# A small triangular solve moved from VectorE to GpSimd in a two-layer encoder kernel

## Chip, cores and metric

One NeuronCore of a Trainium2 chip. The metric is the device time of one execution in microseconds (us), lower is better. The engines are named as the profile names them: PE (TensorE), PEld (its weight loads), DVE (VectorE), ACT (ScalarE), POOL (GpSimd) and SP (SyncE, here a queue of DMAs).

## What is computed

Two layers of an encoder over 512 tokens of width 1024. Each layer projects the tokens, runs five mixers on the result, gates and sums them, projects once more and normalises. Four mixers are attentions. The fifth is a linear recurrence in two directions `e`, and the change lies in it:

```python
def rwkv7_step(state, inp):
    r, w, k, v, a, bb = inp
    sa = jnp.einsum('bhij,bhj->bhi', state, a)
    state = state * w[:, :, None, :] + sa[..., None] * bb[:, :, None, :] + v[..., None] * k[:, :, None, :]
    return state, jnp.einsum('bhij,bhj->bhi', state, r)
...
for e, rev in ((0, False), (1, True)):
    _, ye = lax.scan(rwkv7_step, jnp.zeros((b, B_HEADS, HEAD_DIM, HEAD_DIM), F32), xs, reverse=rev)
```

The kernel doesn't step through 512 tokens. It takes chunks of 64, and inside a chunk the term `sa` makes a triangular system. Its 32x32 diagonal blocks are inverted by substitution, 31 steps long, for all chunks and heads of a unit at once.

## The kernel before

The recurrence of a layer is cut into eight units, four pairs of heads by two directions. A unit has two halves, both generators. `early` makes the decays, the keys and, by PE (line 877), the blocks of the system; ACT copies those out of PSUM into `NS` (lines 886 and 889). `late` turns `NS` into `U` on DVE (line 949), starts `W` from an identity, and runs the substitution: per step a product `pr` (line 959) and a sum into `W` (line 961), 62 instructions a unit, each of which needs the one before. Four DVE transposes bring `W` into the diagonal blocks of `WD` (line 966), one corner of `WD` is cleared (972), two more transposes give `TN` (973), and from there PE and ACT work through the off-diagonal blocks (977, 979, 984, 986), the chunk products (1005 to 1031) and the chain of states (1038 to 1041). The diagonals of the decay, written into `A0` (tile name `AR`, line 929), belong to `early` and are read at line 1023.

The loop over units runs `late(n)` beside `early(n + 1)`, one step of each in turn, and after each step `pull(1)` takes one step of the fill: three matmuls of 512 columns (lines 149 to 151) of the gate and branch products, which have nothing to do with the recurrence. Their weights are split in two parts first, `whi` by ACT (line 135) and `wlo` by DVE (line 136).

The engines' orders are not those of the code. A scheduler works out an order for each engine when the kernel is built, and then it is fixed: each engine takes its instructions one after the other, and one that waits holds up all behind it. POOL before has little to do: DMA issues (lines 365, 434, 436) and a few clears.

Of the kernel before, what the change touches and what calls it, by code (L numbers as in the profile page):

```python
# [14 lines left out]
ALU = mybir.AluOpType  # L15
# [37 lines left out]
def encoder_kernel(ctx: ExitStack, tc: tile.TileContext, x, mem, ln_in, rel_bias, w_in, par, w_up, a_up,  # L53
                   d_lambda, w_mem, w_branch, w_gate, w_out, lnp, cst, cossin, onehot, cnt, msk, out):
    nc = tc.nc
# [26 lines left out]
    tt = nc.vector.tensor_tensor  # L82
# [19 lines left out]
    def M(n):  # L102
        o, w = _MW[n]
        return msk_t[:, o:o + w]
# [167 lines left out]
    with tc.tile_pool(name="init", bufs=1) as ip:  # L272
# [20 lines left out]
        for t in range(2):  # L293
            for j in range(2):
# [4 lines left out]
                sl = slice(t * 128, (t + 1) * 128)  # L299
# [11 lines left out]
        for i in range(2):  # L311
            ps = ps_m()
            sl = slice(i * 512, (i + 1) * 512)
# [10 lines left out]
    for l in range(L):  # L324
# [85 lines left out]
        with tc.tile_pool(name=f"att{l}", bufs=1) as at:  # L410
# [115 lines left out]
            for hp in range(4):  # L526
# [10 lines left out]
                q = q_stack(ps)  # L537
                k = k_stack(ps2)
# [71 lines left out]
            for b in range(4):  # L610
                q = qn
                g = b // 2
                of = tile_of("oc", [128, S], F32, 2)
                for i in range(2):
                    p4 = []
                    for qb in range(4):
                        ps = ps_s()
                        score(ps, q, (kh, kl), i, qb, S, g)
                        p, _ = softmax(ps, S)
# [10 lines left out]
            with tc.tile_pool(name=f"attd{l}", bufs=1) as ad:  # L630
# [12 lines left out]
                for h in range(4):  # L643
                    ps = ps_g()
                    proj(ps, l, 44 + h, hT)
                    q = q_stack(ps)
                    ps = ps_g()
                    proj(ps, l, 48 + h, hT)
                    k = k_stack(ps)
# [5 lines left out]
                    b = load_bias(8 + h)  # L655
# [25 lines left out]
            with tc.tile_pool(name=f"attm{l}", bufs=1) as am:  # L681
                kv = am.tile([128, 4, 256], F32, name="kvm", tag="kvm")
                nc.sync.dma_start(out=kv, in_=scr_kv[l].rearrange("b p t -> p b t"))
                for b in range(2):
                    ps = ps_g()
                    proj(ps, l, 60 + b, hT)
                    q = q_stack(ps)
                    k = k_stack(kv[:, b, :], 256)
                    v = v_pair(kv[:, 2 + b, :], 2)
                    of = tile_of("of", [128, S], F32, 2)  # L690
                    for i in range(2):
                        p4 = []
                        for qb in range(4):
                            ps = ps_s()
                            score(ps, q, k, i, qb, 256)
                            p, _ = softmax(ps, 256, None, (DVE, ACT)[qb % 2])
# [8 lines left out]
        with tc.tile_pool(name=f"rw{l}", bufs=1) as rp:  # L705
            def T(n, shape, bufs=1, dt=F32):
                return rp.tile(shape, dt, name=n, tag=n, bufs=bufs)
# [4 lines left out]
            def recurrence():  # L712
# [10 lines left out]
                WD = T("WD", [128, 8, 128])  # L723
# [74 lines left out]
                def early(p, e):  # L798
                    if e == 0:
                        yield from pair_start(p)  # L800
                    q = pairs[p]
                    up, k, r, v, nkk, vsw, kes = (q[n] for n in ("up", "k", "r", "v", "nkk", "vsw", "kes"))
# [37 lines left out]
                    A0 = T("AR", [128, 8, 3, 64], 2)  # L840
# [17 lines left out]
                    for h in range(2):  # L858
                        sl = slice(64 * h, 64 * h + 64)
# [4 lines left out]
                    Z = T("Z", [128, 2, 4, 128], 2)  # L864
                    OM = T("OM", [128, 2, 8, 128], 2)
                    NS = T("NS", [128, 8, 2, 32], 2)
                    mr = M("mr%d" % e).rearrange("p (o t) -> p o t", o=1).to_broadcast([128, 4, 64])
                    mmk = M("mm%d" % e).rearrange("p (o u t) -> p o u t", o=1, u=2).to_broadcast([128, 2, 2, 64])
                    for c2 in range(2):
                        pss = [ps_s(), ps_m()]  # L870
                        MB = T("MB", [128, 2, 2, 128], 1)
                        for j in range(4):
                            c = 4 * c2 + j
                            for h, ps in enumerate(pss):
                                sl = slice(64 * h, 64 * h + 64)
# [19 lines left out]
                        for h in range(2):  # L895
                            for c in range(2):
# [1 line left out]
                                mm_cols(pmv[:, j * 64:(j + 1) * 64], MB[:, h, c, :], vsw[:, 2 * c2 + c, 64 * h:64 * h + 64])  # L898
                        nc.scalar.copy(Z[:, :, 2 * c2:2 * c2 + 2, 64:128],
                                       pmv[:, 0:256].rearrange("p (h c j) -> p h c j", h=2, j=64))  # L900
                    q[e] = (Z, NS, OM, A0)
                    yield

                    act(comp, comp, AF.Exp, scale=-hc)
# [20 lines left out]
                    for h in range(2):  # L925
                        sl = slice(64 * h, 64 * h + 64)
                        idb = ident[sl, 64 * h:64 * h + 64].rearrange("p (o t) -> p o t", o=1).to_broadcast([64, 8, 64])
                        gcb = gc[sl].rearrange("p (c o) -> p c o", o=1).to_broadcast([64, 8, 64])
                        tt(A0[sl, :, h, :], idb, gcb, ALU.mult)
                    if e == 0:  # L930
                        nc.vector.tensor_copy(kes, ke)
                    else:
# [7 lines left out]

                def late(p, e):
                    q = pairs[p]
                    Z, NS, OM, A0 = q[e]
                    vsw = q["vsw"]


                    U = T("U", [128, 32, 32], 1)
                    nd = NS[:, :, e, :]
                    nc.vector.transpose(out=U, in_=bass.AP(nd.tensor, nd.offset, [list(nd.ap[0]), [1, 32], [64, 8], [0, 4]]))
                    W = T("W", [128, 8, 32], 1)  # L950
                    nc.scalar.copy(W, M("wid").rearrange("p (a b) -> p a b", b=32))
                    for s in range(31, 0, -1) if e == 0 else range(31):
                        if e == 0:
                            t8, rsl, n = slice(s // 4, 8), slice(0, s), s
                        else:
                            t8, rsl, n = slice(0, s // 4 + 1), slice(s + 1, 32), 31 - s
                        nt = t8.stop - t8.start
                        pr = T("pr", [128, 80], 1)[:, :nt * n].rearrange("p (a b) -> p a b", b=n)
                        tt(pr, W[:, t8, s:s + 1].to_broadcast([128, nt, n]),  # L959
                           U[:, s:s + 1, rsl].to_broadcast([128, nt, n]), ALU.mult)  # L960
                        tt(W[:, t8, rsl], W[:, t8, rsl], pr, ALU.add)  # L961
                        if s % 4 == 2:
                            yield
                    for g in range(4):
                        gs = slice(32 * g, 32 * g + 32)
                        nc.vector.transpose(out=WD[gs, :, gs].rearrange("p k (a b) -> p a k b", b=4), in_=W[gs])

                    TN, RB = U[:, 0:8, :], U[:, 8:16, :]
                    sg = [slice(32 * g, 32 * g + 32) for g in (e, 2 + e)]
                    tg = [slice(32 * g, 32 * g + 32) for g in (1 - e, 3 - e)]  # L970
                    for u in range(2):
                        nc.vector.memset(WD[tg[u], :, sg[u]], 0.0)
                        nc.vector.transpose(out=TN[sg[u]], in_=WD[sg[u], :, sg[u]])
                    ps = ps_t()
                    for k in range(8):
# [16 lines left out]
                    n = 0  # L992
# [119 lines left out]
        with tc.tile_pool(name=f"out{l}", bufs=1) as op:  # L1112
# [27 lines left out]
            for t in range(4):  # L1140
                sl = slice(t * 128, (t + 1) * 128)
# [131 lines left out]
```

## Time and profile before

| | |
|---|---|
| median of three runs | 2314.18 us (2313.76 to 2317.56) |
| profiled execution | 2311.92 us, of which the span is 2310.1 us |
| busy share of the span | PE 96%, PEld 73%, DVE 75%, ACT 55%, POOL 3% |
| mean granted clock of PE | 0.991 |

The span reaches from the first to the last instruction. A busy share is the time in which an engine had an instruction in flight. PE's matmuls overlap, so that its share stays high even where they start late.

### The profile page before, as it was taken

The numbers are of one execution on the slowest core, as the hardware profiler recorded it, in microseconds if no ns is written. First come the engines' busy times: TensorE is split into PE (matmuls) and PEld (weight loads), VectorE is DVE, ScalarE is ACT, GpSimd is POOL, SyncE is SP. The second block draws the span as 40 slices with busy tenths as digits, with TensorE's granted clock in tenths as the row PEclk, the third lists the DMA queues.
The fourth block names the chain that finished last, engine by engine and source line by source line (L and its number), as shares of the span: only waits on it lengthen the run. The fifth ranks groups of instructions, "written<-read, shape, count | busy, mean of one in ns | idle before, by whom it ended". The sixth has DMA issues, their size and how long they took to land.

```text
span 2310.1 us, 36289 instructions
## 1 busy us (share of the span) xinstructions
PE 2206.5 (96%) x13056; PEld 1690.5 (73%) x13056; DVE 1733.0 (75%) x4236; ACT 1273.5 (55%) x2785; POOL 60.9 (3%) x119
## 2 busy tenths in 40 slices
PE   6999999999999999999999999999999999999998
PEld 5877777777677777776877777777677777777676
DVE  7676886576889797965567778766778979878455
ACT  3555666675655565544235656666675646555440
POOL 0000000000000000000000000000000000000000
PEclk9999999999999999999999999999999999999999
DMA  7733123332222221315334321232312222222350
GB/s 261 230 95 86 64 76 96 105 95 80 73 79 70 93 77 60 108 51 190 101 116 104 94 64 62 94 99 83 114 60 92 74 65 94 72 93 67 100 180 37
DMA packets 112612, 222.58 MB, mean 96 GB/s; under 512 B 13304, under 2 KB 23288, under 8 KB 112048
## 3 DMA queue, kind: packets, MB, share of 16 engines
q1 hardware_dynamic: 102000, 196.14, 26.5%
q0 software_dynamic: 10432, 24.12, 4.1%
q8 instruction: 103, 1.69, 0.3%
q14 instruction: 77, 0.63, 0.1%
HBM read 188.71 MB, written 28.36 MB: 94 GB/s over the span
## 4 chain that ended last, share of the span: by engine, by line
PE 53%; issue 17%; DVE 17%; ACT 7%; DMA 5%; POOL 0%; SPq 0%; DVEq 0%; POOLq 0%; ACTq 0%
PE pg L150 7%; PE pg L151 7%; PE pg L149 7%; PE pf L149 5%; PE pf L150 4%; PE pf L151 4%; PE psc L443 3%; DVE pr L959 2%; DVE W L961 2%; PE po L488 2%; PE pt L469 2%; DVE wlof L136 1%; PE psc L151 1%; PE psc L150 1%; PE psc L149 1%
## 5 line engine op out<-in xcount | busy, mean ns | idle before, releaser
L150 PE MATMUL pg<-hT,whir 128*128 128x512 f32 (+1 forms) x912 | 366.0, 401 | 0.5 <-DVE hT L176 0.5
L149 PE MATMUL pg<-hT,whir 128*128 128x512 f32 (+1 forms) x912 | 364.4, 400 | 1.9 <-DVE q L424 1.6
L151 PE MATMUL pg<-hT,wlor 128*128 128x512 f32 (+1 forms) x912 | 364.3, 399 | 1.7 <-DVE wlor L136 1.7
L136 DVE TENSOR_TENSOR wlor<-wrawr,whir 128x512 fp32r<-128x512 f32 x240 | 163.7, 687 | 123.2 <-ACT whir L135 114.5
L135 ACT CAST whif<-wrawf 128x512 fp32r<-128x512 f32 (+1 forms) x272 | 164.6, 606 | 149.9 <-PE pf L150 87.4
L135 ACT CAST whir<-wrawr 128x512 fp32r<-128x512 f32 x240 | 147.5, 618 | 178.4 <-PE pg L150 111.9
L149 PE MATMUL pf<-hT,whif 128*128 128x512 f32 x512 | 223.0, 435 | 8.9 <-DVE y L385 5.0
L136 DVE TENSOR_TENSOR wlof<-wrawf,whif 128x512 fp32r<-128x512 f32 (+1 forms) x272 | 181.6, 669 | 48.3 <-ACT whif L135 43.1
L150 PE MATMUL pf<-hT,whif 128*128 128x512 f32 x512 | 208.3, 407 | 0.0
L151 PE MATMUL pf<-hT,wlof 128*128 128x512 f32 x512 | 207.7, 406 | 0.0
L151 PEld LDWEIGHTS pg<-hT,wlor 128*128 128x128 f32 x912 | 172.2, 189 | 40.6 <-DVE wlor L136 4.2
L149 PEld LDWEIGHTS pg<-hT,whir 128*128 128x128 f32 x912 | 172.4, 189 | 38.8 <-ACT whir L135 2.6
L150 PEld LDWEIGHTS pg<-hT,whir 128*128 128x128 f32 x912 | 172.2, 189 | 37.8 <-issue 3.6
L176 DVE TENSOR_TENSOR pT<-pt,pT 128x512 fp32r<-128x512 f32 x176 | 114.2, 686 | 36.3 <-ACT pT L175 34.9
L175 ACT CAST pT<-pt 128x512 fp32r<-128x512 f32 x176 | 94.6, 588 | 63.7 <-PE pt L469 62.6
L149 PEld LDWEIGHTS pf<-hT,whif 128*128 128x128 f32 x512 | 97.5, 190 | 41.2 <-DVE gt L387 10.7
L469 PE MATMUL pt<-cst,p 128*128 128x128 f32 x704 | 118.6, 273 | 0.0
L151 PEld LDWEIGHTS pf<-hT,wlof 128*128 128x128 f32 x512 | 97.3, 190 | 22.4 <-issue 1.6
L959 DVE TENSOR_TENSOR pr<-W,U 128x60 f32<-128x60 f32 (+24 forms) x496 | 103.8, 209 | 11.9
L150 PEld LDWEIGHTS pf<-hT,whif 128*128 128x128 f32 x512 | 98.0, 191 | 18.9 <-issue 3.9
L961 DVE TENSOR_TENSOR W<-W,pr 128x60 f32<-128x60 f32 (+24 forms) x496 | 102.8, 207 | 10.8
L469 PEld LDWEIGHTS pt<-cst,p 128*128 128x128 f32 x704 | 89.7, 141 | 27.3 <-DVE p L460 2.9
(324 smaller groups left out, 4836.9 us busy)
## 6 DMA issues: line engine op xcount, KB each, us to landing
wrawr<-in_w_in_dram SPq DMA_DIRECT2D x224, 256.0 KB, 2.8
wrawf<-in_w_gate_dram SPq DMA_DIRECT2D x160, 256.0 KB, 2.8
o<-scr_o POOLq DMA_DIRECT2D x28, 512.0 KB, 4.5
wrawf<-in_w_branch_dram SPq DMA_DIRECT2D x48, 256.0 KB, 2.7
bias<-scr_toe SPq DMA_DIRECT2D x24, 448.0 KB, 3.3
scr_o<-os SPq DMA_DIRECT2D x20, 512.0 KB, 3.1
wrawf<-in_w_in_dram SPq DMA_DIRECT2D x32, 256.0 KB, 3.2
wrawr<-in_w_out_dram SPq DMA_DIRECT2D x32, 256.0 KB, 3.0
```

The lines of the kernel that those rows point to most:

```text
L135: nc.scalar.copy(hi, raw)
L136: tt(lo, raw, f(hi), ALU.subtract)
L149: mm(ps, ah, bh, start=(i == 0), stop=False)
L150: mm(ps, ah, bl, start=False, stop=False)
L151: mm(ps, al, bh, start=False, stop=(i == n - 1))
L175: nc.scalar.copy(hi, src)
L176: tt(lo, src, f(hi), ALU.subtract)
L443: mm(ps[:, :nk], q[:, i, sl], part[:, i if g is None else g, :nk], start=(j == 0), stop=(j == 1))
L469: nc.tensor.transpose(pt[:, qb * 128:(qb + 1) * 128], p4[qb][:, kb * 128:(kb + 1) * 128], ident)
L488: mm(po, vwin(kb), pT[:, b, :], start=(kb == 0 and b == 0), stop=(kb == nkb - 1 and b == 1))
L959: tt(pr, W[:, t8, s:s + 1].to_broadcast([128, nt, n]), U[:, s:s + 1, rsl].to_broadcast([128, nt, n]), ALU.mult)
L961: tt(W[:, t8, rsl], W[:, t8, rsl], pr, ALU.add)
```

## The change

The substitution and the transpose that feeds it move from the start of `late` into the middle of `early`, right behind the last `NS`, and its 62 instructions go to GpSimd. `late` fetches the result. The transposes that fetch it get a pin: each may not be issued ahead of the DVE instruction traced before it. The clear of the corner and the two diagonals of `A0` go to GpSimd as well. The yields inside the substitution are gone, eight or so a unit, and with them as many steps of the fill in the code's order.

```diff
@@ early @@
+                    U = T("U", [128, 32, 32], 1)
...
-                        tt(pr, W[:, t8, s:s + 1].to_broadcast([128, nt, n]),
+                        nc.gpsimd.tensor_tensor(pr, W[:, t8, s:s + 1].to_broadcast([128, nt, n]),
                            U[:, s:s + 1, rsl].to_broadcast([128, nt, n]), ALU.mult)
-                        tt(W[:, t8, rsl], W[:, t8, rsl], pr, ALU.add)
-                        if s % 4 == 2:
-                            yield
+                        nc.gpsimd.tensor_tensor(W[:, t8, rsl], W[:, t8, rsl], pr, ALU.add)
+                    q[e] = (Z, NS, OM, A0, U, W)
+                    yield
...
-                        tt(A0[sl, :, h, :], idb, gcb, ALU.mult)
+                        nc.gpsimd.tensor_tensor(A0[sl, :, h, :], idb, gcb, ALU.mult)
...
@@ late @@
-                    Z, NS, OM, A0 = q[e]
+                    Z, NS, OM, A0, U, W = q[e]
...
-                        nc.vector.transpose(out=WD[gs, :, gs].rearrange("p k (a b) -> p a k b", b=4), in_=W[gs])
+                        tc.keep_in_program_order(
+                            nc.vector.transpose(out=WD[gs, :, gs].rearrange("p k (a b) -> p a k b", b=4), in_=W[gs]))
...
-                        nc.vector.memset(WD[tg[u], :, sg[u]], 0.0)
+                        nc.gpsimd.memset(WD[tg[u], :, sg[u]], 0.0)
```

In the changed file line 905 is the transpose into `U` (949 before), 915 and 917 are `pr` and `W` (959 and 961), 946 the diagonals (929), 965 the transposes into `WD` (966), 971 the clear, 972 the transposes into `TN` (973) and 976 the first matmuls that need them (977).

The first place is DVE's order in the third unit of layer 0, from the transpose into `U`. Before, the substitution's instructions follow it on the same engine, with other work let in between them:

```order
1065 L949 STREAM_TRANSPOSE U<-NS 128x1024
1066 L959 TENSOR_TENSOR pr<-W,U 128x31
1067 L961 TENSOR_TENSOR W<-W,pr 128x31
1068 L959 TENSOR_TENSOR pr<-W,U 128x30
1069 L961 TENSOR_TENSOR W<-W,pr 128x30
1070 L959 TENSOR_TENSOR pr<-W,U 128x29
```

Now eight instructions (rows with x2 are two) stand between that transpose and the fetch of the result:

```order
929 L905 STREAM_TRANSPOSE U<-NS 128x1024
930 L136 TENSOR_TENSOR wlof<-wrawf,whif 128x512
931 L1040 COPY ST_5177<-pt 64x64
932 L1050 TENSOR_TENSOR SY<-pt,SY 64x256 x2
933 L136 TENSOR_TENSOR wlof<-wrawf,whif 128x512
934 L387 SCALAR_TENSOR_TENSOR gt<-gt,pf 128x512
935 L136 TENSOR_TENSOR wlof<-wrawf,whif 128x512
936 L965 STREAM_TRANSPOSE WD<-W 32x8x8x4 x4
937 L972 STREAM_TRANSPOSE U<-WD 32x256 x2
```

What moved is the whole substitution, and the fetch now follows the transpose closely. Over the eight units of a layer 18, 13, 7, 9, 10, 9, 9 and 11 instructions stand between them.

The second place is PE, in the same unit, where it first needs the result. These are the last rows ahead of it and the first behind:

```order
2490 L149 MATMUL pf<-hT,whif 128x512
2491 L150 MATMUL pf<-hT,whif 128x512
2492 L151 MATMUL pf<-hT,wlof 128x512
2493 L149 MATMUL pf<-hT,whif 128x512
2494 L150 MATMUL pf<-hT,whif 128x512
2495 L976 MATMUL pt<-U,NS 32x32
2496 L151 MATMUL pf<-hT,wlof 128x512
2497 L1066 MATMUL pm<-ys,cst 128x512
2498 L976 MATMUL pt<-U,NS 32x32 x15
```

Between the last block of the system (line 877) and the first matmul of line 976 stood 192, 324, 319, 274, 270, 280, 283 and 204 matmuls in the eight units of a layer before. Now 72, 94, 92, 92, 88, 93, 85 and 105 stand there, of which 48, 27, 52, 40, 48, 43, 45 and 53 have 512 columns.

The third place is POOL, at the head of the same unit's substitution (the rows ahead of it end the unit before):

```order
179 L915 TENSOR_TENSOR pr<-W,U 128x8
180 L917 TENSOR_TENSOR W<-W,pr 128x8
181 L946 TENSOR_TENSOR AR<-cst,gc 64x8x64 x2
182 L971 MEMSET WD 32x8x32 x2
183 L365 DMA o<-scr_o 128x1024 x4
184 L915 TENSOR_TENSOR pr<-W,U 128x31
185 L917 TENSOR_TENSOR W<-W,pr 128x31
```

POOL's queue was nearly empty here; now the diagonals, the clears and the issues of four reloads (line 365, which wait for PE to be done with the tiles that they overwrite) stand between two substitutions.

## Rows read from the trace of the kernel before

**Rows 1.** The page: busy time, share of the span and instructions of each engine.

```profile
span 2310.1 us, 36289 instructions
PE 2206.5 (96%) x13056; PEld 1690.5 (73%) x13056; DVE 1733.0 (75%) x4236; ACT 1273.5 (55%) x2785; POOL 60.9 (3%) x119
```

**Rows 2.** Windows, the two recurrences: width, then busy us (instructions), clock, DMA share, GB/s.

```profile
core 0: us, PE busy (x) PEld busy (x) DVE busy (x) ACT busy (x) POOL busy (x), PEclk, DMA share, GB/s
584.00:1050.00 466.00, 451.81 (x3465) 336.67 (x3464) 384.31 (x1073) 260.44 (x630) 6.48 (x12) 0.99 0.24 76
...
1700.00:2150.00 450.00, 435.28 (x3323) 325.25 (x3322) 382.42 (x1066) 256.83 (x629) 6.49 (x12) 0.99 0.25 77
```

**Rows 3.** Timeline of PE, fill matmuls: start, duration, engine, line, operation, tiles.

```profile
587.83 0.39 PE L149 MATMUL pf<-hT,whif 128*128 128x512 f32 x1
588.06 0.39 PE L150 MATMUL pf<-hT,whif 128*128 128x512 f32 x1
588.29 0.39 PE L151 MATMUL pf<-hT,wlof 128*128 128x512 f32 x1
588.52 0.40 PE L149 MATMUL pf<-hT,whif 128*128 128x512 f32 x1
```

**Rows 4.** Groups by line: what leaves DVE (busy us, mean ns of one).

```profile
L959 DVE TENSOR_TENSOR pr<-W,U 128x60 f32<-128x60 f32 (+24 forms) x496 | 103.8, 209 | 11.9
L961 DVE TENSOR_TENSOR W<-W,pr 128x60 f32<-128x60 f32 (+24 forms) x496 | 102.8, 207 | 10.8
L929 DVE TENSOR_TENSOR AR<-cst,gc 64x512 f32<-64x512 f32 x32 | 21.9, 684 | 0.5
L972 DVE MEMSET WD<- 32x256 f32 x32 | 8.7, 272 | 2.6
```

**Rows 5.** Timeline of DVE: the substitution back to back, layer 0's last unit.

```profile
989.72 0.19 DVE L959 TENSOR_TENSOR pr<-W,U 128x31 f32<-128x31 f32 x1
989.94 0.19 DVE L961 TENSOR_TENSOR W<-W,pr 128x31 f32<-128x31 f32 x1
...
1012.98 0.17 DVE L961 TENSOR_TENSOR W<-W,pr 128x8 f32<-128x8 f32 x1
```

**Rows 6.** Groups by line: what POOL does now.

```profile
L434 POOL DMA_DIRECT2D kh<-kh x40 | 20.7, 517 | 989.8 <-ACT kh L433 805.8 <-DVE wlof L136 125.4 <-PE pt L501 38.9
L321 POOL CAST msk<-mk 128x1152 bf16<-128x1152 f32 x1 | 2.0, 1954 | 21.2 <-DMA par<-in_par_dram 21.2
L724 POOL MEMSET WD<- 128x1024 f32 x2 | 1.9, 973 | 70.0 <-DVE cf L716 35.2 <-DMA scr_o<-os 34.8
L728 POOL MEMSET ST<- 128x128 f32 x4 | 0.8, 229 | 0.0
L1263 POOL MEMSET const-float32-0.0<- 128x1 f32 x1 | 0.1, 98 | 0.2 <-issue 0.2
```

**Rows 7.** Timeline: from the system's blocks to `U`, and from `W` to PE.

```profile
581.09 1.16 PE L877 MATMUL pm<-AR,BK 64*128 64x128 f32 x8
582.51 0.25 ACT L886 COPY NS<-pm 32x128 f32<-32x128 f32 x1
...
583.26 0.20 ACT L889 COPY NS<-pm 32x64 f32<-32x64 f32 x1
584.16 1.24 DVE L949 STREAM_TRANSPOSE U<-NS 128x1024 f32<-128x1024 f32 x1
...
625.33 1.82 DVE L966 STREAM_TRANSPOSE WD<-W 32x256 f32<-32x256 f32 x4
627.18 0.90 DVE L973 STREAM_TRANSPOSE U<-WD 32x256 f32<-32x256 f32 x2
627.67 0.24 PE L977 MATMUL pt<-U,NS 32*32 32x32 f32 x2 [1.92 <-DVE U L973]
```

**Rows 8.** Groups by line: DVE's work that now stands between transpose and fetch.

```profile
L136 DVE TENSOR_TENSOR wlof<-wrawf,whif 128x512 fp32r<-128x512 f32 (+1 forms) x272 | 181.6, 669 | 48.3 <-ACT whif L135 43.1 <-PE pf L151 4.3
L1041 DVE COPY ST<-pt 64x64 f32<-64x64 f32 x112 | 25.4, 227 | 14.7 <-ACT ST L1040 10.9
L1051 DVE TENSOR_TENSOR SY<-pt,SY 64x256 f32<-64x256 f32 x32 | 13.5, 423 | 1.8 <-PE pt L1038 1.2
```

**Rows 9.** Waits of PE for the result: us in total, times, longest.

```profile
PE pt L977 <- DVE U L973: 5.3, 4, 1.9
```

More of the change, by code (lines that the diff above doesn't have):

```diff
@@ L900, in early @@
                                        pmv[:, 0:256].rearrange("p (h c j) -> p h c j", h=2, j=64))
-                    q[e] = (Z, NS, OM, A0)
+                    U = T("U", [128, 32, 32], 1)
+                    nd = NS[:, :, e, :]
+                    nc.vector.transpose(out=U, in_=bass.AP(nd.tensor, nd.offset, [list(nd.ap[0]), [1, 32], [64, 8], [0, 4]]))
+                    W = T("W", [128, 8, 32], 1)
+                    nc.scalar.copy(W, M("wid").rearrange("p (a b) -> p a b", b=32))
+                    for s in range(31, 0, -1) if e == 0 else range(31):
+                        if e == 0:
+                            t8, rsl, n = slice(s // 4, 8), slice(0, s), s
+                        else:
+                            t8, rsl, n = slice(0, s // 4 + 1), slice(s + 1, 32), 31 - s
+                        nt = t8.stop - t8.start
+                        pr = T("pr", [128, 80], 1)[:, :nt * n].rearrange("p (a b) -> p a b", b=n)
+                        nc.gpsimd.tensor_tensor(pr, W[:, t8, s:s + 1].to_broadcast([128, nt, n]),
+                           U[:, s:s + 1, rsl].to_broadcast([128, nt, n]), ALU.mult)
+                        nc.gpsimd.tensor_tensor(W[:, t8, rsl], W[:, t8, rsl], pr, ALU.add)
+                    q[e] = (Z, NS, OM, A0, U, W)
                     yield
@@ L942, in late @@
                     q = pairs[p]
-                    Z, NS, OM, A0 = q[e]
+                    Z, NS, OM, A0, U, W = q[e]
                     vsw = q["vsw"]
[L947 to L958, printed above, removed]
-                        tt(pr, W[:, t8, s:s + 1].to_broadcast([128, nt, n]),
-                           U[:, s:s + 1, rsl].to_broadcast([128, nt, n]), ALU.mult)
-                        tt(W[:, t8, rsl], W[:, t8, rsl], pr, ALU.add)
-                        if s % 4 == 2:
-                            yield
                     for g in range(4):
                         gs = slice(32 * g, 32 * g + 32)
-                        nc.vector.transpose(out=WD[gs, :, gs].rearrange("p k (a b) -> p a k b", b=4), in_=W[gs])
+                        tc.keep_in_program_order(
+                            nc.vector.transpose(out=WD[gs, :, gs].rearrange("p k (a b) -> p a k b", b=4), in_=W[gs]))
                     TN, RB = U[:, 0:8, :], U[:, 8:16, :]
```

## Prediction

> **What bounds the kernel now.** I read the page first: PE is in flight for 96% of the span, DVE for 75%, POOL for 3% [rows 1]. That says little about whether PE is full, so I next looked at starts instead of durations in the timeline. Fill matmuls of 512 columns take 0.39 us each but start 0.23 us apart [rows 3]; back to back they overlap, and 0.23 us is the price of one. Then I took the windows of the two recurrences, the only stretches that the change touches: 466 and 450 us, with PE idle 14.2 and 14.7 us, DVE busy 384 and 382 us (82% and 85%), POOL 6.5 us each [rows 2]. So PE sets the pace there too, DVE is close behind, and all that PE could win back from idleness is 28.9 us, 1.2% of the kernel. PE's waits confirm that the substitution costs it little today: it waits 5.3 us in all, four times, for the transposes that hand the result over [rows 9]. The reason stands in the order: 72 to 105 matmuls stand now, and stood 192 to 324 before, between a unit's last system block and the first matmul that needs the inverse. The long stretch hid a long substitution. The last unit of layer 0 shows how long: from 989.72 to 1013.15 us, 23.4 us with other DVE work in between, where neighbours start 0.22 us apart [rows 5].
>
> **What DVE loses.** 103.8 + 102.8 us of substitution, 21.9 us of diagonals and 8.7 us of clears [rows 4]: 237 us, which takes it from 766 to 529 us of the 916 us in both recurrences, 58%. The gain is what of PE's 28.9 us of idleness was DVE's doing. Some of it is latency from hand to hand that stays, so I take half, 14 us; the ends are 0 and 29 us.
>
> **What the substitution costs on POOL.** 62 instructions, each behind the one before, of 8 to 76 elements a partition; over the 31 steps `nt` times `n` adds up to 1560, 50 on average. No tensor operation with two inputs runs on POOL in this trace, so the price comes from neighbours [rows 6]. A MEMSET of 128 elements takes 0.229 us and one of 1024 takes 0.973 us: 0.83 ns an element and 0.12 us fixed. The CAST of 1152 elements takes 1.954 us: less the fixed part, 1.59 ns for each element read and written. Two inputs read one after the other at that rate make 50 x 2 x 1.59 ns = 0.16 us. DVE's neighbours leave 0.03 us between the end of one and the start of the next [rows 5]. Together 0.31 us. The MEMSET that gave the fixed part reads nothing, and starting two reads is on top, so I take 0.35 us, and 62 x 0.35 = 21.7 us a unit. The low end is the smallest MEMSET, 0.098 us, with 50 elements at 0.83 ns and 0.03 us between: 0.17 us, 10.5 us a unit. The high end is the dearest thing POOL does now, a DMA issue of 0.517 us, with 0.03 us: 0.55 us, 34 us a unit. DVE itself would need 62 x (0.21 + 0.03) = 15 us [rows 4, 5].
>
> The Trainium skill (GPSIMD Engine Reference, section "Performance versus the Vector engine") puts a two-input elementwise operation on GpSimd at about 2.6 cycles an element, about twice VectorE's time, and advises against such work there. By that rate, 50 elements take 0.11 us in place of my 0.16 to 0.20 us, the estimate is 0.26 us an instruction, 16 us a unit, and the sum below would end near 2374 us. No row here can show it.
>
> **How long PE can go without it.** By the order, about 90 matmuls stand between the last system block and the first matmul of line 976, half of them (44.5 on average) of 512 columns: 44.5 x 0.23 = 10.3 us. The other 45 I price by the eight of line 877 that take 1.16 us, 0.27 us of it the last one's own run, so 0.11 us apart [rows 7]: 5.0 us. One us is for small waits of its own, as PE has them now. That makes 16.3 us.
>
> In that time must pass: the copies into `NS`, 0.95 us from the first to the end of the last; the transpose into `U`, 1.24 us; the substitution; four transposes, 1.82 us; the first of two more, 0.44 us; and some 0.35 us of handing over [rows 7]. That is 4.8 us and the substitution.
>
> So PE stands still for the substitution's time less 11.5 us: with 21.7 us, 10.2 us a unit. DVE stands at the pinned fetch meanwhile: it has 7 to 18 instructions ahead of it, mostly of 0.67, 0.42 or 0.23 us [rows 8], 5.8 us on average, and is there first. Behind it wait the weight splits (line 136), so PE would soon starve even if its own next matmul were another. PE takes its instructions in order, so nothing overlaps the wait, and the fill that was meant to hide it is only done later. With 16 units: 163 us. The pin itself costs nothing beyond that, since the fetch can't start before the last sum anyway.
>
> **The smaller parts.** The diagonals on POOL, by the same rates 0.12 + 512 x 2 x 1.59 ns = 1.75 us each, two a unit, stand behind the substitution in six units of eight and are read at line 1022, after two rounds PE to ACT and the chunk products; that cover is some 6 us. Without it the price would be 3.5 us a unit. The clears, 0.3 us each, and the issues of the reloads, 4 x 0.52 us as for line 434, ahead of two units a layer, stand ahead of the substitution and wait for PE, at places near the last system block. I price them at nothing and bound them by 2 us in eight units, 16 us. The missing yields change which fill step stands where, not how many there are: nothing.
>
> **The sum.** The profiled execution took 2311.9 us, its span 2310.1 us, and the median lies 2.3 us above it. 2311.9 + 163 - 14 = 2461; with the 2.3 us, 2463 us, 6.4% slower.
>
> **The rivals.**
> - *POOL is quick enough* (the other side). If an instruction takes less than 0.185 us with its wait, the substitution fits in 11.5 us, PE never waits, and DVE's relief is all that is left: 2300 to 2285 us. Break-even with a gain of 14 us is at 12.4 us a unit, 0.20 us an instruction. For it speaks the low bound; against it, that POOL would have to beat DVE's 0.24 us.
> - *DVE and POOL hold each other up.* If a POOL instruction can't run while DVE reads two operands from SBUF, then the 5.8 us of DVE work ahead of the fetch come on top of the substitution, until DVE itself stands still: 16 x 5.8 = 93 us, 2556 us. The before trace can't tell, as POOL has no such work in it. The Trainium skill (SBUF — State Buffer, section "SBUF: two separate sides") states that rule: a VectorE instruction with two SBUF inputs and a GpSimd one that reads SBUF exclude each other for a whole instruction.
> - *An instruction costs POOL what a DMA issue does*, 0.55 us: 34 - 11.5 = 22.7 us a unit, 363 us, 2663 us.
> - *It does nothing that counts*: the wait and the relief cancel, 0.19 to 0.21 us an instruction, 2310 to 2319 us.
>
> **How the numbers follow.** The forecast's own case, 0.26 to 0.42 us an instruction, 2380 to 2525 us, gets 0.50; with the exclusion 0.20; the dearest POOL 0.11; quick POOL 0.15; cancelled 0.04. Differences under 0.2% (4.6 us) are about what a measurement can't tell from none. The range, 2300 to 2620 us, leaves out a tenth at each side: the better part of the quick case, and the worst of the dear one. Faster 0.15, same 0.04, slower 0.81; the likeliest case alone spans 2380 to 2525 us.
>
> **What the profile after would show.** POOL busy some 300 us more, its lines 915 and 917 starting 0.3 to 0.4 us apart, and a unit's 62 in 19 to 26 us. DVE near 1500 us busy, with idle time ahead of line 965 that is put down to POOL. PE waiting at line 976 for the transposes of 972, sixteen times, 10 us each, with the windows of the two recurrences some 75 us longer apiece and all other windows as they were. If the lines of DVE with two SBUF inputs grow, or POOL's spacing differs between DVE busy and DVE idle, the exclusion is real. I am wrong if POOL's spacing is under 0.2 us, or if PE finds more to do ahead of line 976 than the count of matmuls says, so that its waits there stay short of the substitution less 11.5 us.

## The result, and the profile after

The changed kernel takes 2588.01 us (2587.35 to 2592.86, four runs) against 2315.87 us in the same session: 1.118 times as long, with an interval of 1.1161 to 1.1199. The forecast had 2463 us in a range from 2300 to 2620: slower, as forecast, but by 272 us and not by 149.

The page of the kernel after, its span, its busy shares and the granted clock in 40 slices, beside [rows 1]:

```profile
span 2585.8 us, 36330 instructions
PE 2258.3 (87%) x13056; PEld 1735.2 (67%) x13056; DVE 1563.5 (60%) x3180; ACT 1272.0 (49%) x2785; POOL 420.0 (16%) x1175
PEclk9999999998888888899999999999968898888999
```

DVE is busy 170 us less and POOL 359 us more. TensorE's share falls from 96% to 87%, and in the two recurrences the granted clock leaves the nines. The next rows are windows of layer 0, the recurrence up to its last output and then what is left of the fill behind it, and the two of layer 1 (columns as in [rows 2]):

```profile
540.00:1137.00 597.00, 472.73 (x3502) 355.93 (x3503) 317.99 (x579) 279.82 (x674) 185.82 (x538) 0.87 0.19 58
1137.00:1268.00 131.00, 120.59 (x505) 93.59 (x504) 62.70 (x100) 47.99 (x85) 1.06 (x2) 1.00 0.49 155
1800.00:2400.00 600.00, 476.27 (x3471) 358.34 (x3472) 313.41 (x576) 278.11 (x671) 186.31 (x542) 0.86 0.18 57
2407.00:2538.00 131.00, 121.15 (x508) 93.97 (x507) 60.75 (x97) 45.69 (x81) 1.06 (x2) 1.00 0.43 139
```

PE is in flight for 473 of 597 us, DVE for 318, POOL for 186: no engine is full, so they wait for one another. Measured from a layer's first recurrence instruction to the first normalising step behind the fill, the layers took 595.9 and 598.7 us before and 729.9 and 737.5 us now. That is 134 and 139 us more, 273 in all, of the 276 us between the two profiled spans: nearly the whole loss lies there. What ended the waits of PE, and below of DVE (total us, times, longest), beside [rows 9]:

```profile
PE pt L976 <- DVE U L972: 139.5, 12, 17.7
PE pt L1037 <- DVE ST L1040: 85.7, 18, 12.8
```

```profile
DVE WD L965 <- POOL W L917: 218.4, 16, 17.0
```

DVE stands sixteen times, once a unit, for POOL's last sum. PE stands sixteen times for 10 to 18 us as well, ten times at line 976 and six at line 1037 (the other waits in these two rows are short). One unit shows the first kind. These are the timeline rows of PE in the seventh unit of layer 0 (start, length, then instruction, in brackets the idle time before it):

```profile
1001.46 0.61 PE L877 MATMUL pm<-AR,BK 64*128 64x128 f32 x4
...
1018.14 0.40 PE L796 MATMUL psc<-lowr,uphi 128*128 128x512 f32 x1
1032.96 0.31 PE L976 MATMUL pt<-U,NS 32*32 32x32 f32 x2 [14.43 <-DVE U L972]
...
1035.51 0.63 PE L150 MATMUL pf<-hT,whif 128*128 128x512 f32 x1
1035.94 0.63 PE L151 MATMUL pf<-hT,wlof 128*128 128x512 f32 x1
1036.37 0.63 PE L149 MATMUL pf<-hT,whif 128*128 128x512 f32 x1
```

The same stretch on DVE and then on POOL:

```profile
1005.34 1.24 DVE L905 STREAM_TRANSPOSE U<-NS 128x1024 f32<-128x1024 f32 x1
1006.60 0.23 DVE L1040 COPY ST<-pt 64x64 f32<-64x64 f32 x1
1006.86 0.69 DVE L136 TENSOR_TENSOR wlof<-wrawf,whif 128x512 fp32r<-128x512 f32 x1
1008.22 0.69 DVE L136 TENSOR_TENSOR wlof<-wrawf,whif 128x512 fp32r<-128x512 f32 x1 [0.66 <-ACT whif L135]
...
1013.52 0.80 DVE L389 TENSOR_TENSOR y<-y,gt 128x512 f32<-128x512 f32 x1
1030.62 1.82 DVE L965 STREAM_TRANSPOSE WD<-W 32x256 f32<-32x256 f32 x4 [16.31 <-POOL W L917]
1032.48 0.90 DVE L972 STREAM_TRANSPOSE U<-WD 32x256 f32<-32x256 f32 x2
```

```profile
1006.72 0.24 POOL L915 TENSOR_TENSOR pr<-W,U 128x31 f32<-128x31 f32 x1 [19.77 <-DVE U L905]
1007.03 0.63 POOL L917 TENSOR_TENSOR W<-W,pr 128x31 f32<-128x31 f32 x1
1007.74 0.24 POOL L915 TENSOR_TENSOR pr<-W,U 128x30 f32<-128x30 f32 x1
1008.06 0.25 POOL L917 TENSOR_TENSOR W<-W,pr 128x30 f32<-128x30 f32 x1
1008.39 0.61 POOL L915 TENSOR_TENSOR pr<-W,U 128x29 f32<-128x29 f32 x1
...
1010.40 0.30 POOL L917 TENSOR_TENSOR W<-W,pr 128x54 f32<-128x54 f32 x1
...
1030.38 0.21 POOL L917 TENSOR_TENSOR W<-W,pr 128x8 f32<-128x8 f32 x1
```

The chain is read off directly: POOL runs from 1006.72 to 1030.59 us, the fetch starts at 1030.62, PE's first user at 1032.96. PE had stopped at 1018.5, about 16.5 us after the last system block, and DVE, done at 1014.3, stood ready for the fetch for 16.31 us.

In three units of eight a layer PE meets the second kind of stand. It stops ahead of line 1037, the state chain of the unit before, whose DVE copy is queued behind the fetch. PE and then DVE in the sixth unit:

```profile
932.79 0.40 PE L151 MATMUL pf<-hT,wlof 128*128 128x512 f32 x1
945.35 0.80 PE L1037 MATMUL pt<-ST,PE 128*128 128x128 f32 x2 [12.16 <-DVE ST L1040]
```

```profile
944.16 0.88 DVE L965 STREAM_TRANSPOSE WD<-W 32x256 f32<-32x256 f32 x2 [12.48 <-POOL W L917]
945.07 0.23 DVE L1040 COPY ST<-pt 64x64 f32<-64x64 f32 x1
```

After a stand PE is slow for a while. In the PE rows above, fill matmuls start 0.43 us apart behind the stand, where they started 0.23 us apart in [rows 3]. The windows from ahead of that stand to its end, and two stretches behind, have the granted clock in the third column from the right:

```profile
1004.00:1018.40 14.40, 13.83 (x105) 10.40 (x103) 6.78 (x13) 7.32 (x19) 9.57 (x28) 1.00 0.20 56
1018.40:1033.00 14.60, 0.17 (x2) 0.04 (x2) 2.24 (x6) 0.47 (x2) 9.53 (x35) 0.58 0.00 1
1033.00:1050.00 17.00, 17.00 (x122) 11.63 (x124) 13.42 (x21) 10.85 (x21) 2.60 (x2) 0.66 0.11 32
1050.00:1064.00 14.00, 12.63 (x93) 9.88 (x93) 12.08 (x25) 9.78 (x29) 0.00 (x0) 0.92 0.28 92
```

Between the full level (1.00, 2.4 GHz) and the half one (0.50, 1.2 GHz), 0.66 means 11.6 of 17 us at the half level and 0.92 another 2.2 us of 14. So some 14 us of work ran at half clock behind that stand. It is one of the longer ones: by the same record of the clock it is 4 to 17 us behind the sixteen stands, 9 on average; work at half clock takes nearly twice its time (0.43 against 0.23 us).

From the starts of all of PE's matmuls, with the price of each kind taken from before, the 273 us come apart like this. Gaps of over 1 us grow by 229 us; the sixteen stands are 215 of them. Matmuls that start later than their price while the clock is at its half level take 77 us more. The small waits in between shrink by 34 us, which I put down to DVE's relief. 229 + 77 - 34 = 272. The last two terms depend on where late starts are sorted: a second count, with a median price for each tile and shape and every late start of over 1 us taken as a gap, gives 229 + 69 - 26.

### The profile page after: what moved, and what is told of

Same layout as the page of the kernel before. It is cut to its first block, busy times and chain, and to the rows that moved or that the text cites. A ratio compares the mean times of both kernels' runs of the same rounds, so it can differ in the third digit from the quotient of the medians.

```text
span 2585.8 us, 36330 instructions
## 1 busy us (share of the span) xinstructions
PE 2258.3 (87%) x13056; PEld 1735.2 (67%) x13056; DVE 1563.5 (60%) x3180; ACT 1272.0 (49%) x2785; POOL 420.0 (16%) x1175
## 4 chain that ended last, share of the span: by engine, by line
PE 49%; issue 20%; POOL 13%; DVE 8%; ACT 6%; DMA 3%; SPq 0%; DVEq 0%; POOLq 0%; ACTq 0%
POOL W L917 6%; PE pg L149 6%; PE pg L150 6%; PE pg L151 6%; POOL pr L915 6%; PE pf L149 4%; PE pf L151 4%; PE pf L150 4%; PE psc L443 2%; PE po L488 2%; PE pt L469 2%; PE psc L149 1%; PE psc L151 1%; PE psc L150 1%; PE pt L1004 1%
## 5 line engine op out<-in xcount | busy, mean ns | idle before, releaser
L149 PE MATMUL pf<-hT,whif 128*128 128x512 f32 x512 | 228.9, 447 | 14.1 <-DVE gt L387 8.8
L150 PE MATMUL pf<-hT,whif 128*128 128x512 f32 x512 | 211.4, 413 | 0.0
L434 POOL DMA_DIRECT2D kh<-kh x40 | 20.7, 517 | 992.8 <-ACT kh L433 805.6
L915 POOL TENSOR_TENSOR pr<-W,U 128x60 f32<-128x60 f32 (+24 forms) x496 | 150.6, 304 | 164.2 <-DVE U L905 126.6
L917 POOL TENSOR_TENSOR W<-W,pr 128x60 f32<-128x60 f32 (+24 forms) x496 | 157.4, 317 | 38.8
L965 DVE STREAM_TRANSPOSE WD<-W 32x256 f32<-32x256 f32 x64 | 27.9, 436 | 219.5 <-POOL W L917 218.4
L976 PE MATMUL pt<-U,NS 32*32 32x32 f32 x512 | 20.9, 235 | 139.8 <-DVE U L972 139.5
L149 PEld LDWEIGHTS pf<-hT,whif 128*128 128x128 f32 x512 | 100.4, 196 | 46.0 <-DVE gt L387 15.9
L1037 PE MATMUL pt<-ST,PE 128*128 128x128 f32 x224 | 50.5, 308 | 86.1 <-DVE ST L1040 85.7
```

Of the source, the lines that this page charges most:

```text
L149: mm(ps, ah, bh, start=(i == 0), stop=False)
L150: mm(ps, ah, bl, start=False, stop=False)
L915: nc.gpsimd.tensor_tensor(pr, W[:, t8, s:s + 1].to_broadcast([128, nt, n]), U[:, s:s + 1, rsl].to_broadcast([128, nt, n]), ALU.mult)
L917: nc.gpsimd.tensor_tensor(W[:, t8, rsl], W[:, t8, rsl], pr, ALU.add)
```

## The experiments

Three theories were put to the test. **A**: GpSimd's chain is too long for the distance between the transpose into `U` and the fetch, so DVE stands at the fetch, PE behind DVE, and the half clock follows. **B**: it is the place and the form (early half, pin, missing yields), not the engine. **C**: GpSimd and VectorE shut each other out. Differences are to the kernel before in the same session (medians 2311.8 to 2312.8 us).

| run | time us | to before | ratio, interval |
|---|---|---|---|
| dve_early | 2364.25 | +52 | 1.021 [1.0188, 1.0232] |
| no_pin | 2587.72 | +276 | 1.1185 [1.1163, 1.1206] |
| small_only | 2326.53 | +15 | 1.0053 [1.0034, 1.0072] |
| lag8 | 2370.27 | +58 | 1.0242 [1.0221, 1.0263] |
| half_chain | 2443.08 | +131 | 1.0565 [1.0539, 1.0591] |
| pool_late | 2489.32 | +177 | 1.0766 [1.0739, 1.0793] |
| dve_early_y | 2333.18 | +21 | 1.0091 [1.007, 1.0112] |
| no_yield | 2366.02 | +54 | 1.0239 [1.0213, 1.0265] |
| pool_early_y | 2528.75 | +216 | 1.0921 [1.0884, 1.0959] |
| lag8_dve | 2354.14 | +42 | 1.0178 [1.0158, 1.0199] |
| lag14_dve | 2369.79 | +57 | 1.0241 [1.0223, 1.026] |
| mixed | 2364.98 | +52 | 1.0225 [1.02, 1.025] |

**The engine alone (dve_early).** The changed kernel with the substitution's two lines back on VectorE, still early, without yields, and with a pinned fetch:

```diff
-                        nc.gpsimd.tensor_tensor(pr, W[:, t8, s:s + 1].to_broadcast([128, nt, n]),
+                        tt(pr, W[:, t8, s:s + 1].to_broadcast([128, nt, n]),
                            U[:, s:s + 1, rsl].to_broadcast([128, nt, n]), ALU.mult)
-                        nc.gpsimd.tensor_tensor(W[:, t8, rsl], W[:, t8, rsl], pr, ALU.add)
+                        tt(W[:, t8, rsl], W[:, t8, rsl], pr, ALU.add)
```

> The substitution's 62 instructions go back to VectorE but stay in the early half, behind the pinned fetch; diagonals and clears stay on GpSimd. If the length of the substitution on GpSimd against PE's work ahead of the fetch is the cause (theory A), VectorE's 62 x 0.24 us, spread out again by the scheduler, leave 77 to 134 matmuls of 512 columns ahead of the first user, and the time is 2295 to 2330 us. If the pin or the new place in the code is the cause (B), it stays above 2450 us. If it is the two engines holding each other up at SBUF (C), it is as under A.

Measured 2364 us: 220 of the 272 us go with the engine, and no stand of over 2.1 us is left in the recurrences. At the fetch's user PE now waits:

```profile
PE pt L976 <- DVE U L972: 8.3, 12, 1.4
```

So B alone can't be the main cause. But A had expected the kernel before back, and 52 us stayed; the next runs look for them.

**The pin (no_pin).** The changed kernel with `tc.keep_in_program_order(...)` taken off the fetch.

```diff
-                        tc.keep_in_program_order(
-                            nc.vector.transpose(out=WD[gs, :, gs].rearrange("p k (a b) -> p a k b", b=4), in_=W[gs]))
+                        nc.vector.transpose(out=WD[gs, :, gs].rearrange("p k (a b) -> p a k b", b=4), in_=W[gs])
```

> The changed kernel without the pin on the four fetching transposes. A: the built order differs in the last unit of each layer alone, so 2575 to 2600 us. B, the pin holds VectorE back: below 2450 us.

2587.72 against 2588.01 us: the pin costs nothing.

**The yields (no_yield, dve_early_y).** First the kernel before without the yields in its substitution, then `dve_early` with them put back:

```diff
                        tt(W[:, t8, rsl], W[:, t8, rsl], pr, ALU.add)
-                        if s % 4 == 2:
-                            yield
```

> The kernel before with the seven yields between the substitution's steps left out, nothing else. If yields cost by themselves: 2340 to 2370, with the leftover fill of a layer longer by 15 to 25 us. If they cost nothing, as the prediction has it: 2305 to 2322.

```diff
                         tt(W[:, t8, rsl], W[:, t8, rsl], pr, ALU.add)
+                        if s % 4 == 2:
+                            yield
```

> The changed kernel with the substitution on VectorE in the early half, as in the run of that edit (2364), and with the seven yields between its steps put back. If the missing yields cost the 52 us that run lay above the kernel before (fill that finds no place in the recurrence and runs alone behind it): 2305 to 2335, and the stretch between the last y copy and the first z step falls from 127 to about 78 us a layer. If it is the early place or the small parts on GpSimd: 2350 to 2370, that stretch unchanged.

There are eight yields a unit (every fourth of the 31 steps), not the seven that the recorded texts name. Leaving them out costs the kernel before 54 us, and to put them back gives `dve_early` 31 us. The windows show how, `dve_early` first and then with the yields (recurrence of layer 0, then the fill left over):

```profile
538.00:1034.00 496.00, 468.40 (x3520) 348.53 (x3518) 397.45 (x1077) 284.45 (x680) 32.18 (x44) 0.98 0.22 71
1034.00:1161.00 127.00, 116.78 (x489) 91.19 (x490) 62.18 (x101) 46.12 (x82) 1.06 (x2) 1.00 0.48 157
```

```profile
540.00:1071.00 531.00, 504.24 (x3712) 380.43 (x3711) 423.00 (x1113) 296.12 (x703) 33.39 (x47) 0.98 0.23 74
1071.00:1146.00 75.00, 71.56 (x299) 56.71 (x298) 44.33 (x71) 33.73 (x59) 0.55 (x2) 0.98 0.62 211
```

With the yields PE does 190 matmuls more inside the recurrence and as many fewer behind it. The recurrence grows by 35 us, the rest shrinks by 52. The fill is the same; where it covers the recurrence's waits it costs less than alone.

**The small parts (small_only).** The kernel before, with only the clears and the decay diagonals on GpSimd:

```diff
-                        tt(A0[sl, :, h, :], idb, gcb, ALU.mult)
+                        nc.gpsimd.tensor_tensor(A0[sl, :, h, :], idb, gcb, ALU.mult)
...
-                        nc.vector.memset(WD[tg[u], :, sg[u]], 0.0)
+                        nc.gpsimd.memset(WD[tg[u], :, sg[u]], 0.0)
```

> The kernel before with its diagonals and corner clears alone on GpSimd. A: nothing waits for them, VectorE is 30 us lighter: 2295 to 2318 us. C: thirty-two diagonals of 1.29 us each hold VectorE's two-input instructions up, by up to 41 us: 2320 to 2355 us.

They cost 15 us, though DVE is 30 us freer: 8 us above A's range and within C's. The trace shows C at work. Line 823, a two-input instruction that now often starts beside a diagonal on POOL, takes twice its time, first before and then in `small_only`:

```profile
L823 DVE TENSOR_TENSOR tmp<-tmp 128x512 f32<-128x512 f32 x16 | 11.0, 684 | 0.0
L823 DVE TENSOR_TENSOR tmp<-tmp 128x512 f32<-128x512 f32 x16 | 21.1, 1318 | 0.0
```

Twelve of the sixteen take 1.53 us in place of 0.68. That is 10 us of DVE's time; whether it makes up the 15 us was not shown. With the yields' 31 us the small parts leave 6 of the 52 us of `dve_early` to its early place and the rest, if the three add up.

**Half of the chain (half_chain).** The changed kernel with every second step left out:

```diff
-                    for s in range(31, 0, -1) if e == 0 else range(31):
+                    for s in range(31, 0, -2) if e == 0 else range(0, 31, 2):
```

> Leaves out every second of the 31 steps of the substitution (16 remain, so the inverse is wrong); place, pin and missing yields are those of the changed kernel. GpSimd's chain falls from 23.5 to about 12 us a unit, VectorE's work does not change. Theory A (the stand is the chain less what TensorE has in hand, and the half clock follows the stand): the stands of 10 to 18 us shrink to at most 3 us, the half clock behind them goes, time 2300 to 2360. Theory B (the early place, with the pin and without the yields, costs TensorE its fill whatever the chain's length): above 2500. Theory C (GpSimd and VectorE shut each other out, each busy microsecond alike): half of the 272 us goes, 2440 to 2470.

2443 us, in the range of C and 83 us above that of A. The stands did not shrink to 3 us either: four a layer at line 976 are still 5 to 11 us long. But A's range had left out what the yields and the small parts cost, not known then: with 31 to 54 and 15 us on top it would have been 2346 to 2429. The chain fell from 23 to 24 us to 12 to 13 in most units, and DVE's stand from 218 us to:

```profile
DVE WD L965 <- POOL W L917: 81.5, 14, 10.3
```

That is 8.6 us less a unit for a chain 11 us shorter: the stand follows the chain, though not one for one. A and C can't be told apart by the time of this run.

**The engine in the old place (pool_late).** The kernel before with the two lines on GpSimd, late, with the yields:

```diff
-                        tt(pr, W[:, t8, s:s + 1].to_broadcast([128, nt, n]),
+                        nc.gpsimd.tensor_tensor(pr, W[:, t8, s:s + 1].to_broadcast([128, nt, n]),
                            U[:, s:s + 1, rsl].to_broadcast([128, nt, n]), ALU.mult)
-                        tt(W[:, t8, rsl], W[:, t8, rsl], pr, ALU.add)
+                        nc.gpsimd.tensor_tensor(W[:, t8, rsl], W[:, t8, rsl], pr, ALU.add)
```

> The kernel before with one edit: the substitution's two lines run on GpSimd, in the late half where they stood, with the yields between the steps; clears, diagonals and fetch stay on VectorE, unpinned. Theory A (cover decides, not the engine): the order has 80 to 168 fill matmuls of 512 columns between the last matmul that feeds the chain and its first user in seven units of eight, 18 to 39 us against a chain of 23.5; in the first unit of a layer only 45. So 2320 to 2390, with a stand of about 10 us left in unit 0 of each layer. Theory B (GpSimd itself, through the two engines' shared memory port, sets the time): above 2500, as in the changed kernel.

2489 us: A as it was put, with the count of fill matmuls ahead of PE's first user, missed by 100 us, and B's bound by 11. The timeline of DVE, and then of PE, in one of its units says why:

```profile
716.35 0.70 DVE L136 TENSOR_TENSOR wlof<-wrawf,whif 128x512 fp32r<-128x512 f32 x1 [1.58 <-ACT whif L135]
730.59 1.82 DVE L966 STREAM_TRANSPOSE WD<-W 32x256 f32<-32x256 f32 x4 [13.54 <-POOL W L961]
732.52 0.27 DVE L972 MEMSET WD<- 32x256 f32 x1
732.82 0.76 DVE L1023 TENSOR_TENSOR PE<-pt,AR 128x256 f32<-128x256 f32 x2
```

```profile
718.78 0.39 PE L150 MATMUL pf<-o,whif 128*128 128x512 f32 x1
733.30 1.98 PE L1031 MATMUL pt<-UV,OM 128*64 128x64 f32 x32 [14.13 <-DVE PE L1023]
```

PE wasn't waiting for the inverse. It waited for line 1023, a product of the unit before, which doesn't need the fetched result and stood behind the fetch in DVE's queue. Only two of the sixteen stands here, those of each layer's first unit, are at the result's own user. By the order only 10 to 16 DVE instructions stand between the transpose into `U` and the fetch here, as in the changed kernel (7 to 18). So the cover that counts is that in DVE's queue.

**More room ahead of the fetch (lag8, lag8_dve, lag14_dve).** Empty yields ahead of the fetch in the changed kernel: eight, as many as the substitution had, then eight with the small parts back on DVE, then fourteen likewise.

```diff
                     vsw = q["vsw"]
+                    for _ in range(8):
+                        yield
                     for g in range(4):
```

> The changed kernel, with eight empty steps of the late half ahead of the fetch, so that 56 to 215 matmuls of 512 columns stand ahead of its first user (27 to 53 before). A: 24 us of substitution are covered in nearly all units, the waits of 14 us go, and PE's clock stays up: 2285 to 2330 us. C: the substitution costs the same wherever it is fetched, above 2450 us.

```diff
-                        nc.gpsimd.tensor_tensor(A0[sl, :, h, :], idb, gcb, ALU.mult)
+                        tt(A0[sl, :, h, :], idb, gcb, ALU.mult)
+                    for _ in range(8):
+                        yield
-                        nc.gpsimd.memset(WD[tg[u], :, sg[u]], 0.0)
+                        nc.vector.memset(WD[tg[u], :, sg[u]], 0.0)
```

> The changed kernel with eight empty yields ahead of the fetch, as in the earlier run of that edit (2370), and with the corner clears and decay diagonals back on VectorE. If these small parts cost GpSimd's chain its time: the stand in unit 0 of each layer shrinks from 12 to about 6 us, and the 15 us that they cost alone go: 2330 to 2355. If they are free beside the covered chain: 2365 to 2375.

```diff
-                    for _ in range(8):
+                    for _ in range(14):
                         yield
```

> As the run before it with fourteen empty yields: 56 to 77 instructions between gather and fetch in VectorE's queue in six units of eight, 18 to 36 in the first and the last unit of a layer. If the stands are all that GpSimd costs: TensorE's waits of over 4 us behind the fetch go but for unit 0 and unit 7, 2305 to 2335. If the shared port costs VectorE as much as it is relieved, or the later fetch makes the next steps late: 2340 to 2380, no better than eight.

Eight yields put 26 to 67 DVE instructions between the two, and 214 of the 272 us are gone; the time is still 40 us above A's range, and 80 below C's. DVE stands at the fetch in each layer's first unit alone. PE at the fetch's user:

```profile
PE pt L978 <- DVE U L974: 24.4, 5, 12.3
```

The small parts are worth 16 us again. Fourteen yields are 16 us slower than eight, in the second range of that expectation: the stands in the middle units were gone with eight already, that of the first unit falls from over 12 us to 8.2 and 8.8, the last unit has one of 9.1 us, and a new one comes where a layer's recurrence ends, shown below. What else was seen is the price of GpSimd's instructions, here in `lag8`:

```profile
L917 POOL TENSOR_TENSOR W<-W,pr 128x60 f32<-128x60 f32 (+24 forms) x496 | 182.2, 367 | 38.3
L915 POOL TENSOR_TENSOR pr<-W,U 128x60 f32<-128x60 f32 (+24 forms) x496 | 173.7, 350 | 304.7 <-DVE U L905 267.1
```

and in the changed kernel:

```profile
L917 POOL TENSOR_TENSOR W<-W,pr 128x60 f32<-128x60 f32 (+24 forms) x496 | 157.4, 317 | 38.8
L915 POOL TENSOR_TENSOR pr<-W,U 128x60 f32<-128x60 f32 (+24 forms) x496 | 150.6, 304 | 164.2 <-DVE U L905 126.6
```

The same instructions take 0.05 us longer where DVE works beside them and not stands at the fetch, and a unit's chain is 24.8 to 34.8 us long, not 23 to 24 (30 in the first); the longest has three DMA issues (line 365) in it as well. C is real, then, but small where DVE stands.

**Yields in GpSimd's chain (pool_early_y).** The changed kernel with the eight yields between the steps:

```diff
                         nc.gpsimd.tensor_tensor(W[:, t8, rsl], W[:, t8, rsl], pr, ALU.add)
+                        if s % 4 == 2:
+                            yield
```

> The changed kernel with one edit: the seven yields between the substitution's steps are back, in the early half, the steps still on GpSimd. The order then has 48 to 73 fill matmuls of 512 columns between the last matmul that feeds the chain and its first user (27 to 53 in the changed kernel), but VectorE's queue still has only 9 to 17 instructions between the gather and the fetch (7 to 18). If the stand is set by TensorE's own work up to the first user: 2 to 6 us less a unit, with the yields' own 31 to 54 us, so 2400 to 2480. If it is set by how soon the fetch stands at the head of VectorE's queue, as the run with the substitution on GpSimd in the late half (2489) suggests: only the yields' own price comes back, 2500 to 2560, and TensorE stands at the state chain, not at the fetch's user.

2529 us, 59 less: the yields' own price and little more, as expected if DVE's queue decides. The second half of that expectation missed: 154 us of PE's waits are at the fetch's user and 35 at the state chain. And the sixteen stands are 36 us shorter in all, 2.2 us a unit, the low end of what the other branch had; only the time speaks for DVE's queue here, and `pool_late` is the clearer run.

**Each engine where it fits (mixed).** As `lag14_dve`, but the first and the last unit of a layer do their substitution on VectorE, late, with yields.

```diff
+                    on_v = (p, e) in (units[0], units[-1])
...
-                    for _ in range(14):
-                        yield
+                    if on_v:
...
+                            tt(pr, W[:, t8, s:s + 1].to_broadcast([128, nt, n]),
...
+                    else:
+                        for _ in range(14):
+                            yield
```

> As the run with fourteen yields and the small parts on VectorE, but in the first and the last unit of a layer, where there is too little to cover GpSimd's chain, the substitution is that of the kernel before (VectorE, late half, with its seven yields). If the stands of those two units (8.4, 9.2 and 11.2 us a layer) and the half clock behind them are what that run still lost: they go, 57 us of it, and with VectorE relieved in twelve units of sixteen the time is 2290 to 2312, at or below the kernel before. If GpSimd's work beside VectorE's costs by itself (longer instructions on both through the shared port): 2320 to 2350.

2365 us, above both ranges: the stands of the two units are gone, and only 5 us with them. PE's waits show the one that comes with fourteen yields:

```profile
PE psc L149 <- ACT gt L379: 20.6, 2, 10.3
```

It is there with the same numbers in `lag14_dve` and not in `lag8`. So the first version that beats the kernel before, if there is one, would need its room ahead of the fetch without that wait; it wasn't tried. What `mixed` takes more than the kernel before lies in the recurrences: a layer has 22 us more in gaps of over 1 us, half of it that wait, 11 to 13 more at half clock, and 6 less in small waits. Which of the later fetch and of the longer instructions on both engines makes the other gaps was not settled.

## Why the prediction was right in kind, and which terms were off

The time lies in the stated range because that was wide. The forecast's own case, 0.26 to 0.42 us an instruction, held the instruction (0.39 us with the distance to the next) but not the time, which lies 63 us above that case's 2525. The upper part of the range had been kept for the exclusion (2556) and a dearer POOL, and neither made most of the loss.

**The stand at the fetch: right in kind, forecast a quarter short.** It was 10.2 us a unit, the substitution and 4.8 us of steps less 16.3 us of work. The stands add up to 215 us, 13.4 a unit, in place of 163. *TensorE's work*: from the start of the last matmul of line 877 to that of the last one ahead of the stand it is 14.9 to 19.5 us in the sixteen units, 17.1 on average. *The substitution*: 21.7 us became 23.0 to 24.0, and 29.9 in the first unit of a layer; 24.4 on average. In that unit two diagonals in between cost 3 us, and DVE has the most work ahead of its fetch there, beside which POOL's instructions take 3 to 4 us longer in sum. An instruction takes 0.31 us with 0.08 us to the next one's start, 0.39 on average, against 0.35. *The steps around it*: the transpose into `U` starts 2.0 to 4.5 us after the start of the last system block, because DVE has masks and, in three units of eight, state copies to do first; I had counted only the copies into `NS`, 0.95 us, though [rows 7] have 1.9 us from the end of the last block to the transpose. That made 2 us a unit. In the units whose stand ends at the state chain PE is let go about a microsecond sooner. That PE waits for DVE's queue and not for its own operand, as it does in these six of sixteen units, was named in the prediction, though with the weight splits as the first to be missed; it is the state copy (1040).

**The clock: a term that was not there.** Work at the half level behind the stands took 77 us longer (69 by the second count), a third on top of them. The sum priced every matmul at its full-clock distance.

**DVE's relief: 26 to 34 us by the two counts, not 14,** if all of the shrinking is its doing, which was not shown. By the second count the small waits are 22, 12 and 10 us less than before in `lag8_dve`, `lag14_dve` and `mixed`, with DVE relieved and few stands; the rest may come from the stands themselves, in which ACT and DVE get ahead of PE. The bound of 29 us was the idle time of [rows 2], which are 916 us of the two layers' 1195 and leave out PE's late starts while it counts as busy.

**The missing yields: not nothing.** 54 us in the kernel before, 31 and 59 us in two versions of the changed one. The sentence that they change which fill step stands where, not how many there are, is true, and the cost is in the where. I take them as no further term, since the stands and the clock already fill the sum: their fill is part of the work that PE lacked ahead of the stands, and with it back in `pool_early_y` the stands are 2.2 us a unit shorter.

**The small parts: 15 and 16 us,** the upper bound and not the nothing that was taken. **The pin: nothing,** as taken.

**The rivals.** Quick POOL and cancelling are refuted by 0.37 us from start to start in the median. The DMA-like price, 0.55 us, is as well (its sum was 34 less 11.5, 22.5 us a unit and not 22.7; and by the same sum 0.26 to 0.42 us an instruction would be 2374 to 2533 us, not 2380 to 2525). The exclusion between DVE and POOL exists: in the POOL rows above, the instructions that start at 1007.03 and 1008.39 us take 0.63 and 0.61 us, beside line 136 on DVE from 1006.86 and 1008.22, and end 0.1 us behind it; their neighbours take 0.24. The Trainium skill (SBUF — State Buffer, section "SBUF: two separate sides") has such a pair of instructions exclude each other for a whole instruction, and the trace agrees in these rows. The prediction priced it at 5.8 us a unit. Of the 992 instructions, 100 ran beside a two-input DVE instruction and took 0.544 us, 780 beside an idle DVE and took 0.282: 26.5 us, 1.7 a unit. I take it to stay small because DVE soon stands at the fetch; `lag8`, where DVE doesn't, has longer ones. The DVE lines grow too, as the prediction asked: line 823 takes 1.11 us on average in place of 0.68.

The Trainium skill (GPSIMD Engine Reference, section "Performance versus the Vector engine") has a rate an element, by which the prediction's estimate was 16 us a unit and 2374 us. The rows show 0.21 us for 8 elements and 0.28 to 0.30 us for 54, 1.5 to 2 ns an element, near the 2.2 ns of that estimate; the 0.20 us that each instruction takes besides makes the chain long.

## What to carry to other kernels

When a serial chain moves to another engine, compare its length (instructions times the distance from start to start) with the work that stands between issue and fetch in the queue of the engine that fetches. TensorE's fill covers only up to the first thing that it needs out of the queue that stands; that came ahead of the result's own user in six of sixteen units here, and in fourteen in `pool_late`. Price a stand of TensorE with the half clock behind it, here a third on top. And code that was cut into steps to let other work in has a cover to lose even where every step is kept.

## What the runs showed of the hardware that was not expected

- The granted clock fell to its half level during each of the sixteen stands of 10 to 18 us and stayed there for 4 to 17 us of work behind them, some 14 behind the one shown. In the kernel before, each recurrence had 7 us at the half level; after, 150 and 171 us, the stands themselves included.
- A dependent instruction on GpSimd starts 0.08 us after the end of the one before, on VectorE 0.03 us [rows 5], by the profile's spans. Over 62 instructions that is 3 us of the 8 or 9 that the chain is longer than the prediction's 15 us for VectorE.
- The diagonals, 512 elements a partition, take 1.29 us on GpSimd, not the 1.75 us that was worked out from a CAST and two MEMSETs:

```profile
L946 POOL TENSOR_TENSOR AR<-cst,gc 64x512 f32<-64x512 f32 x32 | 41.2, 1287 | 160.7 <-ACT gc L819 159.4
```
